# Convolution halves delayed, block sums written earlier, and one block fewer in the second up group of an encoder trunk

## The chip, the cores and the metric

The kernel runs on one core of one Trainium2 chip. The metric is the device time of one execution in microseconds; lower is better. TensorE is called PE here, VectorE DVE, ScalarE ACT, GpSimd POOL and SyncE SP, as in the profile.

## The reference, cut to what matters

Two encoder layers over 256 tokens of 2048 features. Each has an attention mixer and then a gated feed-forward network with a convolution along the tokens; the change touches only the latter.

```python
D_MODEL = 2048; SEQ = 256; DEPTH = 2; D_FF = 5632; CONV_W = 3
...
def conv_ffn(x, w_up, conv_w, conv_b, w_down):
    h = jnp.einsum("bsd,df->bsf", x, w_up)
    g, u = h[..., :D_FF], h[..., D_FF:]
    gp = jnp.pad(g, ((0, 0), (1, 1), (0, 0)))
    g = conv_w[0] * gp[:, :-2] + conv_w[1] * gp[:, 1:-1] + conv_w[2] * gp[:, 2:] + conv_b
    return jnp.einsum("bsf,fd->bsd", jax.nn.gelu(g) * u, w_down)
...
for layer in range(DEPTH):
    ...
    f = conv_ffn(rmsnorm(h, ln_ffn[layer]), ffn_w_up[layer], ffn_conv_w[layer],
                 ffn_conv_b[layer], ffn_w_down[layer])
    h = h + f.astype(h.dtype)
```

## The kernel before, in words

**Products in three matmuls.** Every float32 operand is split into a rounded high part and the rest, the low part. A product is high x high, high x low and low x high: three matmuls (L195 to L197, or `products`, L874 to L877). A weight comes in units of 256 rows by 512 columns: SP loads it into `raw` (a ring of 5 buffers, L124), ACT casts it into `wh`, DVE subtracts and writes `wl` (rings of 4; `split`, L230 to L234). A unit makes 12 matmuls of 512 columns: two row tiles, two token halves, three matmuls each.

**Up groups.** The 5632 gate and 5632 value columns are worked off in 11 groups `j` of 512 and 512 (`up_group`, L922). In a group the first half, `x = 0`, makes the gate columns in two PSUM banks, one for each 128 tokens, and the second half, `x = 1`, the value columns. When a half is done, ACT writes it scaled into `z` (L953), DVE turns `z` in 32 x 32 pieces (L279) and 16 small DMAs, four from SP and twelve from POOL, move the pieces to their places, so that features lie on the partitions (`qk`).

**Blocks.** In groups 1 to 10 the units `u` of `UPK` (1 and 3) don't go as plain units. `up_front` (L844) makes for each of them a block of 2 x 2 tiles with seven products instead of eight: `front_forms` (L887) loads the unit's gate and value weights, DVE makes sums of them (L894 to L901), and four products go into four banks of the next group while the current group still runs (`block`, L850; 12 matmuls). `merged` (L858) then adds these banks up (DVE L862 to L866, ACT L861 and L865) and writes the sums back as the starting values of the next group. That group begins with `up_direct` (L915), which loads the unit's value weight once more and adds the three products left (9 matmuls). The first block is called as `up_front` starts, in the gate half before the third last unit, the second at the same place of the value half.

**The order of the work.** `later(delay, fn)` puts a function off by so many ticks; `tick()` (L98) is called after every second unit and runs what is due. The convolution of a group (`convolved`, L963) is done in two halves of two feature tiles: ACT makes the middle tap and the bias (L971), DVE adds the other two taps (L972, L974), ACT takes the gelu (L977). It needs the gate half's `qk`. `multiplied` (L1001) then multiplies gate and value (L1004) and splits the products for the down projection. The program is written in this order, and a scheduler then places the instructions of each engine; an engine does what it has in its fixed order, so an instruction that waits holds up all behind it.

**Down projection.** Groups 0 to 5 and 6 to 10 make two halves of a layer (`HALVES`), and after each the products are multiplied by the down weights (`pair_head`, L1075), with blocks of their own (`column_forms`, L1012; `seven_products`, L1042). So the last group of a half, 5 or 10, finishes its convolution and `multiplied` during `pair_head`. There are four such ends in the kernel.

Of the kernel before, what the change touches and what calls it, by code (L numbers as in the profile page):

```python
# [48 lines left out]
AHEAD = 4  # L49
LAST = 2  # L50
UPK = (1, 3)
HALVES = ((0, 6, (1, 2, 3)), (6, 11, (1, 2, 3)))


# [17 lines left out]
def trunk_kernel(ctx: ExitStack, tc, a, out):  # L72
# [21 lines left out]
    def later(delay, fn, rank=2):  # L94

        pending.append((now[0] + delay, rank, fn))
# [212 lines left out]
    def turned_rows(c, gain, res):  # L309
# [6 lines left out]
        def tiles():  # L316
            for j in range(4):
                res[c * 4 + j] = y_tile(pf.rearrange("p (t j) q -> p j t q", t=2)[:, j], gain, c * 4 + j)
            for n, u in enumerate(UPK):
                if res is formed.get("of") and c == u // 2:  # L320
# [240 lines left out]
    ps = tps("s", 2)  # L561
# [273 lines left out]
    for pair in range(2):  # L835
        ps, vt = gemm_a(a["evb_v"][pair], yT, KT), []
# [7 lines left out]
    def up_front(layer, j, yT):  # L844

        gm = (j >= HALVES[0][1]) == j % 2
        b1, b7, b6, b5 = (tps(*(("gm", 4) if gm else (tag, 2))) for tag in ("s", "s", "tp", "tp"))
        direct = []

        def block(n):  # L850
            u = UPK[n]
            w11, t1, t2, t3, t4 = front_forms([a["up"][layer, j, x] for x in range(2)], u, j)
            s1, s2, s3, s4 = formed[u]
            for ps, form, w in ((b1, token_block(yT, 2 * u, 0), w11), (b7, s3, t3), (b6, s2, t2), (b5, s1, t1)):
                products(ps, form, w, n == 0, u == UPK[-1])
            direct.append((u, s4, t4))

        def merged():  # L858

            s1, x0, x1 = (tmp.tile([P, 512], F32, name=nm("sum"), tag=tag) for tag in ("rx", "ry", "ry"))  # L860
            S.copy(s1, b1)  # L861
            V.tensor_tensor(x0, s1, b6, op=ALU.add)  # L862
            V.tensor_tensor(x1, x0, b7, op=ALU.add)
            V.tensor_tensor(b6, x0, b5, op=ALU.add)
            S.copy(b7, x1)  # L865
            V.tensor_tensor(b5, x1, b5, op=ALU.add)  # L866

        block(0)
        return [[b1, b7], [b6, b5]], direct, merged, block

    def token_block(act, kt, t):
        return [act[kt][:, x, t * P:(t + 1) * P] for x in range(2)]
# [1 line left out]
    def products(ps, form, w, first=False, last=False, onto=False):  # L874
        (ah, al), (wh, wl) = form, w
        for i, (x, y) in enumerate(((ah, wh), (ah, wl), (al, wh))):
            T.matmul(ps, x, y, start=first and i == 0, stop=last and i == 2, skip_group_check=onto)  # L877
# [44 lines left out]
    def up_group(layer, j, yT, rstd, prod, front, after, *more):  # L922

        sides = {}
        src = [a["up"][layer, j, x] for x in range(2)]
        if front:
            pss, direct = front[:2]
            units = [u for u in range(8) if u not in UPK]
            for u, s4, t4 in direct:
                up_direct(pss, src, yT, u, s4, t4)  # L930
        else:
            pss = [[tps("gm", 4), tps("gm", 4)] for _ in range(2)]
            units = list(range(8))
        nxt = None
        for x in range(2):
            for n, u in enumerate(units):
                if not j and not x and u == 2:
                    rstd.append(row_factor())
                if not x and u == units[-3] and after:
                    nxt = up_front(*after)  # L940
                if x and nxt and u == units[-3]:
                    nxt[3](1)
                if front:
                    own_unit(pss[x], src[x], u, yT, u == units[-1])
                else:
                    a_unit(pss[x], src[x], u, yT, KT)
                if n % 2 == 1 or n == len(units) - 1 and n % 2 == 0:
                    tick()
            if x and nxt:
                nxt[2]()  # L950
            z = new_z("f k")
            for t in range(2):
                S.activation(z.rearrange("p (f t) k -> p t f k", t=2)[:, t],  # L953
                             pss[x][t].rearrange("p (f k) -> p f k", k=P), AF.Copy, scale=rstd[0][:, t:t + 1])
            sides[x] = quad(2 * x)
            turned(z.rearrange("p b k -> p (b k)"), sides[x].rearrange("p f (t k) -> p (f t) k", k=P), (3,))
            if not x:
                later(2, lambda: convolved(layer, j, sides, 0))
                later(4, lambda: convolved(layer, j, sides, 1))
        later(3, lambda: multiplied(j, sides, prod, *more))  # L960
        return nxt

    def convolved(layer, j, sides, part):  # L963

        if not part:
            sides[2] = quad(4)
        g4, c4 = sides[0], sides[2]
        for i in (2 * part, 2 * part + 1):
            f = 4 * j + i
            g, c = g4[:, i, :], c4[:, i, :]  # L970
            S.activation(c, g, AF.Identity, scale=convw[:, layer, 1, f:f + 1], bias=convb[:, layer, f:f + 1])  # L971
            V.scalar_tensor_tensor(c[:, 1:SEQ], g[:, 0:SEQ - 1], convw[:, layer, 0, f:f + 1],  # L972
                                   c[:, 1:SEQ], op0=ALU.mult, op1=ALU.add)
            V.scalar_tensor_tensor(c[:, 0:SEQ - 1], g[:, 1:SEQ], convw[:, layer, 2, f:f + 1],  # L974
                                   c[:, 0:SEQ - 1], op0=ALU.mult, op1=ALU.add)
        half = c4[:, 2 * part:2 * part + 2, :]
        S.activation(half, half, AF.Gelu_apprx_tanh)  # L977
# [115 lines left out]
    def chunk_pair(src, c, act, forms, nk, done, after=None):  # L1093

        nu = nk // 2
        nxt = None
        heads = nu - 3 if nu > 10 else nu - 2
        pss = pair_head(src, c, act, forms, sorted(forms), heads, nk)
        if not c:
            flush()  # L1100
        for x in range(2):
            for u in range(heads, nu):
                if not x and u == nu - 1 and after:
                    nxt = up_front(*after)
                if x and nxt and u == nu - 2:
                    nxt[3](1)
                a_unit(pss[x], src[c + x], u, act, nk)
            if x and nxt:
                nxt[2]()
            if c:  # L1110
                tick()
            done(pss[x], c + x)
        return nxt
# [111 lines left out]
    ps = gemm_a(a["odc"][0], yT, KT, hooks={6: flush})  # L1225
# [10 lines left out]
    for n in range(2):  # L1236
        ps = gemm_a(a["odc"][1 + n], yT, KT)
# [6 lines left out]
    for hh in range(2):  # L1244
        vt = v_tiles(gemm_a(a["od_v"][hh], yT, KT), rstd, ((18, 19, 20, 21), (16, 17, 22, 23))[hh])
        for hd in range(hh * 4, hh * 4 + 4):
            y = att.tile([P, 6, 64], F32, name=nm("nb"), tag="bias", bufs=2)
# [167 lines left out]
def _paired_up(w):  # L1415

    w = w.copy()
    for u in UPK:
        x, y = w[:, 1:, 0, u].copy(), w[:, 1:, 1, u].copy()
        w[:, 1:, 0, u] = np.concatenate([x[..., :512], y[..., :512]], axis=-1)  # L1420
        w[:, 1:, 1, u] = np.concatenate([y[..., 512:], x[..., 512:]], axis=-1)
    return w


# [69 lines left out]
```

## Time and profile before

| | |
|---|---|
| median of 3 runs | 2425.67 us (2424.55 to 2427.95) |
| profiled execution | 2421.42 us |
| its span, first to last instruction | 2419.6 us |
| granted PE clock, mean | 0.997 |
| PE busy | 2386.3 us, 10841 matmuls |
| DVE, ACT, POOL busy | 1874.3, 1409.4, 537.4 us |
| weights and the rest from HBM | 479.46 MB, 199 GB/s over the span |

Rows of a timeline hold the start in us, the duration, the engine, the source line, the operation, what it writes and reads, its shape and count, and in brackets the idle time of the engine before it with what ended that. Rows of one kind that follow each other are merged and counted (x4). SPq is SP's queue, in which DMAs are started. Rows of waits read: who waited, for whom, total us, times, the longest. Rows of windows read: the window, its length, then busy time and count of PE, of its weight loads, of DVE, ACT and POOL, then the granted clock, the share of the DMA engines, and GB/s.

### The profile page before, as it was taken

The page shows a single profiled execution, that of the slowest core. Times are in us where ns is not written, and L with a number is a line of the kernel's source. Part 1 is how long each engine was busy: PE and PEld are TensorE (multiplying, and loading weights), DVE is VectorE, ACT ScalarE, POOL GpSimd, SP SyncE. Part 2 cuts the span into 40 slices and gives each one's busy share as a digit, 9 for nine tenths or more (in the row PEclk, how much of TensorE's full clock was granted, in tenths as well). Part 3 has the DMA queues.
Part 4 walks back from the last instruction along what each step waited for, and adds up shares of the span by engine and source line. Part 5 has one row for each costly group of instructions (what it writes and reads, how often), then busy time and mean ns, then how long its engine had stood idle before and what let it go on. Part 6 is the DMA issues. An engine that isn't in the chain of part 4 may idle for free.

```text
span 2419.6 us, 33368 instructions
## 1 busy us (share of the span) xinstructions
PE 2386.3 (99%) x10841; PEld 1974.4 (82%) x10841; DVE 1874.3 (77%) x2525; ACT 1409.4 (58%) x2078; POOL 537.4 (22%) x940
## 2 busy tenths in 40 slices
PE   9999999999999999999999999999999999999998
PEld 7888888888877887888887888888788878887877
DVE  6576566766778987798978867777788877989787
ACT  7455455566656665456655667555566554566554
POOL 1132032322222332002331200322223320033310
PEclk9999999999999999999999999999999999999999
DMA  8778678766767887678877754667688866788864
GB/s 307 204 194 238 199 193 239 219 195 188 218 203 245 246 248 201 199 231 247 250 227 202 234 183 141 196 192 218 194 254 244 251 192 200 234 236 242 244 202 156
DMA packets 293295, 526.65 MB, mean 218 GB/s; under 512 B 159736, under 2 KB 161144, under 8 KB 293120
## 3 DMA queue, kind: packets, MB, share of 16 engines
q1 hardware_dynamic: 262608, 491.12, 64.7%
q0 software_dynamic: 30080, 32.74, 7.9%
q8 instruction: 85, 1.39, 0.2%
q14 instruction: 90, 0.74, 0.1%
q10 hardware_dynamic: 432, 0.66, 0.1%
HBM read 479.46 MB, written 2.18 MB: 199 GB/s over the span
## 4 chain that ended last, share of the span: by engine, by line
PE 65%; DMA 12%; DVE 11%; issue 4%; POOL 4%; ACT 2%; SPq 2%; DVEq 0%; ACTq 0%; POOLq 0%
PE gm L196 14%; PE gm L195 14%; PE gm L197 14%; DMA qk<-z 9%; PE gm L877 5%; DVE wl L234 5%; PE s L877 4%; POOL qk L273 4%; PE tp L877 3%; PE gm L145 2%; DMA raw<-in_up 2%; SPq L273 2%; DVE z L279 1%; PE gm L150 1%; DVE qk L972 1%
## 5 line engine op out<-in xcount | busy, mean ns | idle before, releaser
L231 ACT CAST wh<-raw 128x1024 fp32r<-128x1024 f32 (+1 forms) x915 | 931.2, 1027 | 680.5 <-PE gm L197 346.4
L234 DVE TENSOR_TENSOR wl<-raw,wh 128x1024 fp32r<-128x1024 f32 (+1 forms) x915 | 1080.2, 1194 | 285.1 <-ACT wh L231 275.3
L273 POOL DMA_DIRECT2D qk<-z x656 | 377.3, 583 | 1129.4 <-DVE z L279 1079.9
L196 PE MATMUL gm<-wl,yT 128*128 128x512 f32 x988 | 385.5, 390 | 1.6 <-DVE wl L234 1.6
L195 PE MATMUL gm<-wh,yT 128*128 128x512 f32 x988 | 386.7, 392 | 0.0
L197 PE MATMUL gm<-wh,yT 128*128 128x512 f32 x988 | 385.3, 390 | 0.0
L877 PE MATMUL gm<-wh,yT 128*128 128x512 f32 x832 | 265.8, 390 | 0.0
L877 PE MATMUL s<-wh,yT 128*128 128x512 f32 x672 | 218.5, 390 | 0.0
L196 PEld LDWEIGHTS gm<-wl,yT 128*128 128x128 f32 x988 | 185.7, 188 | 39.9 <-DVE wl L234 2.7
L197 PEld LDWEIGHTS gm<-wh,yT 128*128 128x128 f32 x988 | 185.5, 188 | 39.0 <-DVE yT L240 0.2
L195 PEld LDWEIGHTS gm<-wh,yT 128*128 128x128 f32 x988 | 185.6, 188 | 37.8 <-issue 0.4
L196 PE MATMUL gm<-wl,prod 128*128 128x512 f32 x518 | 204.3, 394 | 9.3 <-DVE wl L234 9.3
L195 PE MATMUL gm<-wh,prod 128*128 128x512 f32 x518 | 203.6, 393 | 2.8 <-ACT wh L231 2.8
L197 PE MATMUL gm<-wh,prod 128*128 128x512 f32 x518 | 203.4, 393 | 0.0
L877 PEld LDWEIGHTS gm<-wh,yT 128*128 128x128 f32 x832 | 156.2, 188 | 32.9
L877 PE MATMUL tp<-wh,yT 128*128 128x512 f32 x576 | 180.6, 389 | 0.0
L877 PE MATMUL gm<-wl,yT 128*128 128x512 f32 x416 | 162.6, 391 | 0.7 <-DVE wl L234 0.7
L877 PEld LDWEIGHTS s<-wh,yT 128*128 128x128 f32 x672 | 126.2, 188 | 26.7
L877 PE MATMUL s<-wl,yT 128*128 128x512 f32 x336 | 131.4, 391 | 0.0
L877 PEld LDWEIGHTS tp<-wh,yT 128*128 128x128 f32 x576 | 108.1, 188 | 22.4
L196 PEld LDWEIGHTS gm<-wl,prod 128*128 128x128 f32 x518 | 98.3, 190 | 32.4 <-DVE wl L234 12.0
L195 PEld LDWEIGHTS gm<-wh,prod 128*128 128x128 f32 x518 | 98.2, 190 | 24.6 <-ACT wh L231 4.0
(386 smaller groups left out, 3645.9 us busy)
## 6 DMA issues: line engine op xcount, KB each, us to landing
raw<-in_up SPq DMA_DIRECT2D x392, 512.0 KB, 4.9
raw<-in_down SPq DMA_DIRECT2D x176, 512.0 KB, 4.4
raw<-in_eva_qk SPq DMA_DIRECT2D x96, 512.0 KB, 4.4
raw<-in_eva_v SPq DMA_DIRECT2D x46, 512.0 KB, 5.9
qk<-z POOLq DMA_DIRECT2D x656, 32.0 KB, 3.9
raw<-in_evb_qk SPq DMA_DIRECT2D x32, 512.0 KB, 4.7
raw<-in_ev_out SPq DMA_DIRECT2D x32, 512.0 KB, 4.2
raw<-in_od_qk SPq DMA_DIRECT2D x32, 512.0 KB, 4.3
```

The costliest lines, as they stand in the source:

```text
L145: T.matmul(ps.rearrange("p a b -> p (a b)"), wh[:, k * P:(k + 1) * P], act[u * 8 + k].rearrange("p a b -> p (a b)"), start=(u == 0 and k = ...
L150: T.matmul(ps[:, 1, :], wl[:, k * P:(k + 1) * P], act[u * 8 + k][:, 0, :], start=False, stop=(u * 8 + k == KT - 1))
L195: T.matmul(ps[t], ah, wh[:, sl], start=(kt == 0), stop=False)
L196: T.matmul(ps[t], ah, wl[:, sl], start=False, stop=False)
L197: T.matmul(ps[t], al, wh[:, sl], start=False, stop=(kt == nk - 1))
L231: first = S.copy(dst_h, src)
L234: V.tensor_tensor(dst_l, src, dst_h.bitcast(F32), op=ALU.subtract)
L273: (nc.sync if i in on_sync else G).dma_start(dst[j * 32:(j + 1) * 32, :, i * 32:(i + 1) * 32], z[i * 32:(i + 1) * 32].rearrange("p (b j c) ...
L279: V.transpose(p, p)
L877: T.matmul(ps, x, y, start=first and i == 0, stop=last and i == 2, skip_group_check=onto)
L972: V.scalar_tensor_tensor(c[:, 1:SEQ], g[:, 0:SEQ - 1], convw[:, layer, 0, f:f + 1], c[:, 1:SEQ], op0=ALU.mult, op1=ALU.add)
```

## The change

Three edits. First, a function `blocks(j)` takes the place of `UPK`: group 1 has one block, of unit 3, and unit 1 is a plain unit of it; its block is made in the value half of group 0, and nothing in the gate half. Group 1 has seven plain units in each half then, and four ticks instead of three. Second, `merged` is called before the tick behind the last unit of the value half instead of after it, ahead of what that tick has due. Third, the two halves of the convolution are due 3 and 4 ticks after the gate half instead of 2 and 4, and 4 and 5 in the last group of a half.

```diff
+def blocks(j):
+    return () if j == 0 else UPK[1:] if j == 1 else UPK
...
+        us = blocks(j)
+
         def block(n):
-            u = UPK[n]
+            u = us[n]
...
-                products(ps, form, w, n == 0, u == UPK[-1])
+                products(ps, form, w, n == 0, u == us[-1])
...
-        block(0)
-        return [[b1, b7], [b6, b5]], direct, merged, block
+        return [[b1, b7], [b6, b5]], direct, merged, block, len(us)
...
-            units = [u for u in range(8) if u not in UPK]
+            units = [u for u in range(8) if u not in blocks(j)]
...
                     nxt = up_front(*after)
+                    if nxt[4] > 1:
+                        nxt[3](0)
                 if x and nxt and u == units[-3]:
-                    nxt[3](1)
+                    nxt[3](nxt[4] - 1)
...
-                if n % 2 == 1 or n == len(units) - 1 and n % 2 == 0:
+                if x and nxt and u == units[-1]:
+                    nxt[2]()
+                if n % 2 == 1 or u == units[-1]:
                     tick()
-            if x and nxt:
-                nxt[2]()
...
-                later(2, lambda: convolved(layer, j, sides, 0))
-                later(4, lambda: convolved(layer, j, sides, 1))
+                for part in range(2):
+                    later(part + (3 if after else 4), lambda part=part: convolved(layer, j, sides, part))
```

The weights are stored accordingly (`_paired_up`), and `chunk_pair` calls the first block of group 6 itself.

What it does to the order is shown by the rows of the instructions as they are placed. The lines of the change are 4 to 9 higher; L978 to L984 are its convolution, L1011 its product of gate and value, L1034 to L1038 its sums of down weights. Numbers behind a name are buffers.

First place: DVE at the end of the first half of layer 0, where the convolution of group 5 (`qk`) and the turn of its values (`z`) stand beside the first down weights (`raw`, `wl`). Before:

```order
L234 TENSOR_TENSOR wl_8506<-raw_8503,wh_8505 128x1024
L972 SCALAR_TENSOR_TENSOR qk_8416<-qk_8326,convw,qk_8416 128x255
L974 SCALAR_TENSOR_TENSOR qk_8416<-qk_8326,convw,qk_8416 128x255
L972 SCALAR_TENSOR_TENSOR qk_8416<-qk_8326,convw,qk_8416 128x255 x2
L974 SCALAR_TENSOR_TENSOR qk_8416<-qk_8326,convw,qk_8416 128x255 x2
L972 SCALAR_TENSOR_TENSOR qk_8416<-qk_8326,convw,qk_8416 128x255
L1027 TENSOR_TENSOR t_1576_8619<-raw_8615 128x512
L974 SCALAR_TENSOR_TENSOR qk_8416<-qk_8326,convw,qk_8416 128x255
L234 TENSOR_TENSOR wl_8531<-raw_8528,wh_8530 128x1024
L279 STREAM_TRANSPOSE z_8460<-z_8460 128x1024
```

With the change:

```order
L238 TENSOR_TENSOR wl_8485<-raw_8482,wh_8484 128x1024
L979 SCALAR_TENSOR_TENSOR qk_8500<-qk_8313,convw,qk_8500 128x255
L981 SCALAR_TENSOR_TENSOR qk_8500<-qk_8313,convw,qk_8500 128x255
L979 SCALAR_TENSOR_TENSOR qk_8500<-qk_8313,convw,qk_8500 128x255
L981 SCALAR_TENSOR_TENSOR qk_8500<-qk_8313,convw,qk_8500 128x255
L238 TENSOR_TENSOR wl_8511<-raw_8508,wh_8510 128x1024
L1034 TENSOR_TENSOR t_1571_8606<-raw_8602 128x512
L283 STREAM_TRANSPOSE z_8439<-z_8439 128x1024
L238 TENSOR_TENSOR wl_8529<-raw_8526,wh_8528 128x1024
L979 SCALAR_TENSOR_TENSOR qk_8500<-qk_8313,convw,qk_8500 128x255 x2
L981 SCALAR_TENSOR_TENSOR qk_8500<-qk_8313,convw,qk_8500 128x255 x2
```

The second half of the convolution has moved behind one weight, the turn of `z` and another weight. A little further on in the same place, before:

```order
L1031 TENSOR_TENSOR raw_8616<-raw_8616 128x512
L234 TENSOR_TENSOR wl_8629<-raw_8615,wh_8628 128x1024
L1027 TENSOR_TENSOR t_1593_8701<-raw_8697 128x512
L234 TENSOR_TENSOR wl_8637<-raw_8616,wh_8636 128x1024
L1004 TENSOR_TENSOR qk_8416<-qk_8416,qk_8463 128x1024
L1028 TENSOR_TENSOR raw_8697<-raw_8698,raw_8697 128x512
L234 TENSOR_TENSOR wl_8664<-raw_8661,wh_8663 128x1024
```

With the change:

```order
L1038 TENSOR_TENSOR raw_8603<-raw_8603 128x512
L238 TENSOR_TENSOR wl_8616<-raw_8602,wh_8615 128x1024
L1034 TENSOR_TENSOR t_1588_8688<-raw_8684 128x512
L1011 TENSOR_TENSOR qk_8500<-qk_8500,qk_8442 128x1024
L238 TENSOR_TENSOR wl_8624<-raw_8603,wh_8623 128x1024
L238 TENSOR_TENSOR prod_8588<-qk_8500,prod_8588 128x256 x2
L238 TENSOR_TENSOR prod_8593<-qk_8500,prod_8593 128x256 x2
L238 TENSOR_TENSOR wl_8651<-raw_8648,wh_8650 128x1024
```

The product of gate and value now comes before the weight that follows the subtraction, and the four splits of the products before the next weight. The other three ends have the same order.

Second place: DVE from group 1 to group 2 of layer 0; `sum` and `gm` are the sums of group 2's blocks, `wl_6946` before and `wl_6940` now are its first direct weight. Before:

```order
L862 TENSOR_TENSOR sum_6914<-sum_6913,gm_6638 128x512
L234 TENSOR_TENSOR wl_6898<-raw_6895,wh_6897 128x1024
L863 TENSOR_TENSOR sum_6915<-sum_6914,gm_6637 128x512
L864 TENSOR_TENSOR gm_6638<-sum_6914,gm_6639 128x512
L866 TENSOR_TENSOR gm_6639<-sum_6915,gm_6639 128x512
L234 TENSOR_TENSOR wl_6946<-raw_6943,wh_6945 128x1024
L972 SCALAR_TENSOR_TENSOR qk_6869<-qk_6744,convw,qk_6869 128x255 x2
L974 SCALAR_TENSOR_TENSOR qk_6869<-qk_6744,convw,qk_6869 128x255 x2
```

With the change:

```order
L868 TENSOR_TENSOR sum_6901<-sum_6900,gm_6607 128x512
L238 TENSOR_TENSOR wl_6885<-raw_6882,wh_6884 128x1024
L979 SCALAR_TENSOR_TENSOR qk_6874<-qk_6713,convw,qk_6874 128x255 x2
L981 SCALAR_TENSOR_TENSOR qk_6874<-qk_6713,convw,qk_6874 128x255 x2
L869 TENSOR_TENSOR sum_6902<-sum_6901,gm_6606 128x512
L870 TENSOR_TENSOR gm_6607<-sum_6901,gm_6608 128x512
L872 TENSOR_TENSOR gm_6608<-sum_6902,gm_6608 128x512
L979 SCALAR_TENSOR_TENSOR qk_6874<-qk_6713,convw,qk_6874 128x255 x2
L981 SCALAR_TENSOR_TENSOR qk_6874<-qk_6713,convw,qk_6874 128x255 x2
L238 TENSOR_TENSOR wl_6940<-raw_6937,wh_6939 128x1024
```

Both halves of group 1's convolution now stand before the direct weight, and the first of them before three of the sums.

Third place: DVE from group 0 to group 1 of layer 0. Before:

```order
L972 SCALAR_TENSOR_TENSOR qk_6400<-qk_6310,convw,qk_6400 128x255
L974 SCALAR_TENSOR_TENSOR qk_6400<-qk_6310,convw,qk_6400 128x255
L972 SCALAR_TENSOR_TENSOR qk_6400<-qk_6310,convw,qk_6400 128x255
L862 TENSOR_TENSOR sum_6523<-sum_6522,tp_6217 128x512
L974 SCALAR_TENSOR_TENSOR qk_6400<-qk_6310,convw,qk_6400 128x255
L863 TENSOR_TENSOR sum_6524<-sum_6523,s_6216 128x512
L864 TENSOR_TENSOR tp_6217<-sum_6523,tp_6218 128x512
L866 TENSOR_TENSOR tp_6218<-sum_6524,tp_6218 128x512
L234 TENSOR_TENSOR wl_6555<-raw_6552,wh_6554 128x1024
```

With the change:

```order
L868 TENSOR_TENSOR sum_6482<-sum_6481,tp_6217 128x512
L979 SCALAR_TENSOR_TENSOR qk_6437<-qk_6276,convw,qk_6437 128x255
L869 TENSOR_TENSOR sum_6483<-sum_6482,s_6216 128x512
L870 TENSOR_TENSOR tp_6217<-sum_6482,tp_6218 128x512
L872 TENSOR_TENSOR tp_6218<-sum_6483,tp_6218 128x512
L981 SCALAR_TENSOR_TENSOR qk_6437<-qk_6276,convw,qk_6437 128x255
L979 SCALAR_TENSOR_TENSOR qk_6437<-qk_6276,convw,qk_6437 128x255
L238 TENSOR_TENSOR wl_6521<-raw_6518,wh_6520 128x1024
```

The sums begin before the second half of the convolution instead of within it; one step of it stands behind the direct weight.

More of the change, by code (lines that the diff above doesn't have):

```diff
@@ L1104, in chunk_pair @@
                     nxt = up_front(*after)
+                    nxt[3](0)
                 if x and nxt and u == nu - 2:
@@ L1417, in _paired_up @@
     w = w.copy()
[L1418 to L1421, printed above, removed]
+    for j in range(w.shape[1]):
+        for u in blocks(j):
+            x, y = w[:, j, 0, u].copy(), w[:, j, 1, u].copy()
+            w[:, j, 0, u] = np.concatenate([x[..., :512], y[..., :512]], axis=-1)
+            w[:, j, 1, u] = np.concatenate([y[..., 512:], x[..., 512:]], axis=-1)
     return w
```

## The prediction

> **What bounds the kernel now.** I read the page first, then PE's waits, then the stretches by window, and last the timelines of PE, ACT, DVE and SP where PE waits.
>
> ```profile
> span 2419.6 us, 33368 instructions
> PE 2386.3 (99%) x10841; PEld 1974.4 (82%) x10841; DVE 1874.3 (77%) x2525; ACT 1409.4 (58%) x2078; POOL 537.4 (22%) x940
> PE gm L196 <- DVE wl L234: 11.6, 10, 1.8
> 1956.00:1966.00 10.00, 7.39 (x25) 5.40 (x24) 10.00 (x15) 7.74 (x11) 4.79 (x9) 0.83 0.49 95
> 2306.00:2317.00 11.00, 8.13 (x22) 6.24 (x23) 10.47 (x15) 7.29 (x10) 6.23 (x11) 0.69 0.50 112
> ```
>
> PE is busy 99% of the span, so time is lost only in single waits. The third line (source, what it waited for, us, times, longest) says what for: the low part of a weight that DVE subtracts. The last two lines (PE, PEld, DVE and ACT busy, then the granted clock) are stretches with such waits in which the clock fell as well. The profiled execution took 2421.42 us, 1.8 us more than its span and 4.25 us less than the median of the runs, 2425.67.
>
> The same thing happens at the end of every half of a layer, at four places. Here is the first, on PE, then ACT, DVE and SP:
>
> ```profile
> 921.32 0.39 PE L195 MATMUL gm<-wh,prod 128*128 128x512 f32 x1
> ...
> 926.76 0.39 PE L195 MATMUL gm<-wh,prod 128*128 128x512 f32 x1
> 927.74 0.50 PE L196 MATMUL gm<-wl,prod 128*128 128x512 f32 x1 [0.59 <-DVE wl L234]
> ...
> 943.09 0.50 PE L1054 MATMUL tp<-wl,form 128*128 128x512 f32 x1 [0.73 <-DVE wl L234]
> ...
> 946.49 0.51 PE L196 MATMUL gm<-wl,prod 128*128 128x512 f32 x1 [1.75 <-DVE wl L234]
> ...
> 955.92 0.50 PE L1054 MATMUL tp<-qk,form 128*128 128x512 f32 x1 [0.25 <-DVE qk L234]
> ```
>
> ```profile
> 921.94 2.08 ACT L971 ACTIVATE qk<-qk,convb,convw 128x256 f32<-128x256 f32 x4 [4.81 <-DMA qk<-z]
> 924.50 1.04 ACT L231 CAST wh<-raw 128x1024 fp32r<-128x1024 f32 x1
> ```
>
> ```profile
> 922.57 0.48 DVE L972 SCALAR_TENSOR_TENSOR qk<-qk,convw,qk 128x255 f32<-128x255 f32 x1 [4.18 <-ACT qk L971]
> ...
> 926.46 1.22 DVE L234 TENSOR_TENSOR wl<-raw,wh 128x1024 fp32r<-128x1024 f32 x1
> 927.59 1.24 DVE L279 STREAM_TRANSPOSE z<-z 128x1024 f32<-128x1024 f32 x1
> ...
> 941.20 0.69 DVE L1027 TENSOR_TENSOR t<-raw 128x512 f32<-128x512 f32 x1 [4.06 <-DMA raw<-in_down]
> 941.81 1.22 DVE L234 TENSOR_TENSOR wl<-raw,wh 128x1024 fp32r<-128x1024 f32 x1
> 943.47 1.22 DVE L1004 TENSOR_TENSOR qk<-qk,qk 128x1024 f32<-128x1024 f32 x1 [0.44 <-issue]
> ...
> 945.22 1.22 DVE L234 TENSOR_TENSOR wl<-raw,wh 128x1024 fp32r<-128x1024 f32 x1
> ```
>
> ```profile
> 928.86 2.55 SPq L273 DMA_DIRECT2D qk<-z  x4
> 931.52 1.27 SPq L128 DMA_DIRECT2D raw<-in_down  x2
> 932.91 0.39 SPq L1015 DMA_DIRECT2D raw<-in_down  x1
> ```
>
> 24 matmuls of 512 columns start in 926.76 - 921.32 us, so one costs 0.227 us, not its 0.39 of duration. ACT stands 4.81 us before the convolution's first step, whose gates, transposed and moved by DMA, have not landed, and every cast of a weight stands behind it. DVE then runs all eight steps of the convolution (922.57 to 926.46 with one subtraction of a weight between) before the weight that PE wants at 926.99. That is the first wait. DVE's backlog delays z, SP's four moves of z stand ahead of the next weights, and 13 us later DVE waits 4.06 us for a weight; PE waits twice more, until 946.49, and shortly at 955.92.
>
> **The change part by part.**
>
> *One block instead of two in group 1.* Per layer PE loses 12 matmuls of the block and 9 of its direct products, and gains 24 of two plain units: 3 more, 6 in all, 6 x 0.227 = **+1.4 us**. PE is the bound, so nothing hides them. In return DVE does 7 steps fewer a layer and SP starts one load fewer, and the block's two loads no longer stand in group 0's queue. PE has no wait there in this trace, so that saving is hidden behind PE and I take it at nothing; what it could do for the stream of loads is a rival.
>
> *Sums ahead of due work, group 0 to group 1.*
>
> ```profile
> 707.56 1.08 ACT L971 ACTIVATE qk<-qk,convb,convw 128x256 f32<-128x256 f32 x2
> 708.55 0.56 ACT L861 COPY sum<-s 128x512 f32<-128x512 f32 x1
> 709.50 0.68 DVE L862 TENSOR_TENSOR sum<-sum,tp 128x512 f32<-128x512 f32 x1
> 712.28 2.35 DVE L234 TENSOR_TENSOR wl<-raw,wh 128x1024 fp32r<-128x1024 f32 x2
> 713.56 0.50 PE L877 MATMUL tp<-wl,form 128*128 128x512 f32 x1 [1.16 <-DVE wl L234]
> ```
>
> In the new order ACT copies the sum before the second pair of convolution steps, so at 707.56, done at 708.1. Four sums at 0.6 apart and the three steps left at 0.4 then bring DVE to the weight, done at 708.1 + 2.4 + 1.2 + 1.2 = 712.9 instead of 713.45: 0.55 us of PE's wait goes, in both layers **-1.1 us** (0 if the sums come no earlier).
>
> *The same edit and the later halves, group 1 to group 2.* With a second plain unit, group 1's second half is longer, and the new order has the convolution ahead of the direct block's weight, where it stood behind it.
>
> ```profile
> 736.90 0.69 ACT L953 ACTIVATE z<-s,rstd 128x512 f32<-128x512 f32 x1 [0.67 <-PE s L877]
> 750.86 1.22 DVE L234 TENSOR_TENSOR wl<-raw,wh 128x1024 fp32r<-128x1024 f32 x1
> 755.04 0.98 DVE L972 SCALAR_TENSOR_TENSOR qk<-qk,convw,qk 128x255 f32<-128x255 f32 x2 [2.96 <-DMA raw<-in_up]
> 755.74 0.39 PE L877 MATMUL gm<-wh,form 128*128 128x512 f32 x1
> PE gm L877 <- DVE wl L234: 0.7, 1, 0.7
> ```
>
> The gate half ends on PE at about 736.75, where z could start. Six units of 12 matmuls and a block of 12 later, 84 x 0.227 = 19.1 us, PE begins the direct products (755.74); the weight was made at 750.86. Now PE comes there 7 units and a block, 96 x 0.227 = 21.8 us after the gate half, and needs the weight's low part at 22.0. DVE starts the convolution, if its gates land as before, at 755.04, 18.3 us after the gate half, and puts four steps (1.7), three sums (1.8), four steps (1.6) and the weight (1.2) in a row: 24.5 us. ACT's cast of the same weight stands behind its own four steps too, but ends before the sums do. PE, with the direct products of two blocks queued behind the one that waits, stands 2.4 us, in two layers **+4.8 us**. Ends: 0, if the gates land 2.5 us sooner, to +3 a layer. In the first layer a later wait of 0.7 (last line, between 755 and 800 us) has that slack, **-0.7 us**.
>
> *The halves one tick later, at the four ends.* Now four steps stand before the weight and four behind z. DVE gets to the weight after 1.7 us instead of 3.9, so 2.2 us sooner, at 925.5 done: the wait at 926.76 goes. ACT's pair, cast and z let DVE turn z at 926.0 instead of 927.59, so SP's moves and the weights behind them start 1.6 us sooner, and the weight at 941.20, which lands behind those in one stream, at 939.6. POOL's twelve moves of the same z keep their order and start 1.6 us sooner as well. But there the new order is worse: behind that subtraction now stand L1004, the weight, the four products and the next weight (0.6 + 1.1 + 1.1 + 1.4 + 1.2 = 5.4 us), where the last low part was done 946.44 - 941.20 = 5.2 us behind it. At the first place L1004 waits for its own z besides: it started at 943.47, so now at 941.9, and what stands from there to the second weight takes 4.8 us, to 946.7 and not 946.44. PE's first wait is given back to the later ones (2.7 and 1.1 us, 1.4 apart, in place of 0.9 and 1.9): 0.25 us lost, 0.4 gained at 955.92, for which the weights now stand earlier, 0.2 us gained in all. The other places:
>
> ```profile
> 1285.16 0.69 DVE L1027 TENSOR_TENSOR t<-raw 128x512 f32<-128x512 f32 x1 [4.05 <-DMA raw<-in_down]
> 1288.64 1.22 DVE L234 TENSOR_TENSOR wl<-raw,wh 128x1024 fp32r<-128x1024 f32 x1
> 1973.43 0.69 DVE L1027 TENSOR_TENSOR t<-raw 128x512 f32<-128x512 f32 x1 [4.13 <-DMA raw<-in_down]
> 1976.92 1.22 DVE L234 TENSOR_TENSOR wl<-raw,wh 128x1024 fp32r<-128x1024 f32 x1
> 2309.38 0.80 PE L196 MATMUL gm<-wl,prod 128*128 128x512 f32 x1 [1.66 <-DVE wl L234]
> 2322.25 0.69 DVE L1027 TENSOR_TENSOR t<-raw 128x512 f32<-128x512 f32 x1 [2.21 <-DMA raw<-in_down]
> 2327.95 0.39 PE L196 MATMUL gm<-wl,prod 128*128 128x512 f32 x1
> ```
>
> At the second and third the weight was done 4.7 us behind the subtraction; 5.4 us behind one that is 1.6 us sooner gains 0.9 each, and 0.4 for the short wait behind. At the fourth the first wait, ended at 2309.38, ends 1.9 us sooner, and the second barely takes from it (2322.25 - 1.6 + 5.4 = 2326.05, against PE's 2327.95, the row that wanted that weight). Sum 0.2 + 1.3 + 1.3 + 1.9 = **-4.7 us**. Ends: 0, if the weight lands no sooner, to -8, if the second waits shrank like the first. Between, from group 2's value half to group 4 and in groups 6 to 9, the order does not move, so the edits cost and gain nothing there.
>
> Sum: 1.4 - 1.1 + 4.8 - 0.7 - 4.7 = -0.3 us, 2421.1 against 2421.42 of the profiled execution, and with the same difference against the median **2425.4 us**: no change.
>
> **A rule weighed.** The clock fell to 0.69 around 2306 to 2317, though no wait of L196 in PE's list passed 1.8 us: the one of 1.66 us at 2309.38 stood close behind another. The new order makes the second waits longer (2.7 and 1.1 us at the first end). The Trainium skill, TensorE: Matmul & The Clock Gate, Part 1, lets the clock fall only after an idle window of about 3.4 us; no wait that I expect is as long, so by the page it never falls at the ends and the sum stays. The trace disagrees with its number and decides: a fall is a rival.
>
> **The rivals.** *Slower, A: the weights land no sooner.* The load that DVE waits for at 941.20 reuses a buffer that the moved order frees no earlier than before. If it is its own issue that counts and not the stream ahead of it, the ends give 0: 1.4 - 1.1 + 4.8 - 0.7 = +4.4, with 3 instead of 2.4 us at group 2 +5.6: 2431.3 us. It decides from under 0.5 us of shift. For it: SP starts that load at 932.91 now, and in the new order I get 932.8. Against: two loads were started within 1.27 us ahead of it, and DVE had it only 8.3 us after its start, so they come one behind the other. Chance 0.18. *Slower, B: the clock falls* at three of four ends, 2 us each (0.31 of the clock over the 11 us of the window above would be 3.4, half of it behind waits): -0.3 + 6 = +5.7, 2431.4 us. Chance 0.08. *Faster: no wait at group 2*, because the gates land sooner with a weight less in the stream, -4.8: -5.1, 2420.6 us. Chance 0.22. *The change does nothing* is inside the forecast, 0.52.
>
> **How the numbers follow.** Two measurements tell about 0.2% apart, 4.9 us. The rivals' ends give the chances: faster 0.22, same 0.52, slower 0.26. The range reaches from 2418 (the faster rival with 2 us more at the ends) to 2432 (A with a fall of the clock).
>
> **What would show it.** PE's list: the wait at the first low part of each end gone, the one at L1054 about 2 us, and a new wait of about 2.4 us on `gm<-wl,form` at group 2. ACT's 4.8 us before the convolution stays. Wrong would be: group 2 without a wait, the subtraction at the ends as late as now, or a clock under 0.9 at three ends.

## The result, and the profile after

The changed kernel takes 2435.72 us (median of 5 runs, 2432.66 to 2440.45) against 2425.67 us before. The ratio of the runs is 1.0053, 95% interval 1.0037 to 1.0069. A second set of runs (e9 below) gave 2435.03 against 2422.60 us, ratio 1.0050 (1.0033 to 1.0066). So the change costs 10 to 12 us where the prediction had 0 and reached up to 2432. Single runs of one kernel lie up to 15 us apart (before, in the 30 runs beside e1 to e4: 2415.95 to 2431.40), so medians of many runs and ratios decide, and a single profile is good for the place of a loss, not for its last microsecond.

The head of the page after, and its list of PE's waits (source, what it waited for, total us, times, longest):

```profile
span 2433.7 us, 33342 instructions
PE 2392.7 (98%) x10847; PEld 1978.6 (81%) x10847; DVE 1867.5 (77%) x2511; ACT 1406.4 (58%) x2072; POOL 538.7 (22%) x940
```

```profile
PE tp L1061 <- DVE wl L238: 6.4, 4, 2.9
PE gm L200 <- DVE wl L238: 6.4, 8, 1.2
PE gm L882 <- DVE wl L238: 5.9, 3, 2.7
PE tp L882 <- DVE wl L238: 5.3, 5, 1.8
PE gm L882 <- DVE gm L870: 3.4, 2, 2.4
```

PE has the six matmuls more. L200 (the L196 of before) waits half as long, L1061 (L1054) four times as long (6.4 us in four waits, where about 2 us each were forecast); new are 5.9 + 3.4 us on `gm` at L882, the direct products of group 2.

To see where the time went I take, for every matmul of a trace, the distance to the next one's start less the median distance for its width (0.227 us at 512 columns), and add this up over stretches between the same points of the program. The same points are the same matmuls in the order of the program, which hardly differs between the kernels. What PE loses so contains its waits and the slower pace behind them, in us:

| | group 0 to 1, both layers | group 1 to 2, both layers | four half-ends | the rest | all |
|---|---|---|---|---|---|
| before | 5.5 | 2.1 | 23.1 | 23.0 | 53.7 |
| after | 5.8 | 13.9 | 20.9 | 25.7 | 66.3 |
| after, again (e9) | 7.1 | 14.0 | 20.2 | 24.3 | 65.6 |

12.6 us of loss and 6 x 0.227 = 1.4 us of matmuls make 14.0 of the 14.1 us between the two spans. 11.8 of them lie at one place: the end of group 1. There, in the first layer, on PE, DVE and ACT of the changed kernel:

```profile
755.13 0.39 PE L882 MATMUL tp<-wh,yT 128*128 128x512 f32 x1
757.91 0.47 PE L882 MATMUL gm<-wh,form 128*128 128x512 f32 x1 [2.40 <-DVE gm L870]
761.13 0.80 PE L882 MATMUL gm<-wl,form 128*128 128x512 f32 x1 [2.74 <-DVE wl L238]
```

```profile
737.19 0.69 DVE L900 TENSOR_TENSOR raw<-raw,raw 128x512 f32<-128x512 f32 x1 [0.92 <-DMA raw<-in_up]
...
738.53 1.24 DVE L283 STREAM_TRANSPOSE z<-z 128x1024 f32<-128x1024 f32 x1
...
748.66 1.23 DVE L238 TENSOR_TENSOR wl<-raw,wh 128x1024 fp32r<-128x1024 f32 x1 [1.03 <-ACT wh L235]
754.80 0.98 DVE L979 SCALAR_TENSOR_TENSOR qk<-qk,convw,qk 128x255 f32<-128x255 f32 x2 [4.91 <-DMA raw<-in_up]
755.69 0.87 DVE L981 SCALAR_TENSOR_TENSOR qk<-qk,convw,qk 128x255 f32<-128x255 f32 x2
756.49 0.68 DVE L869 TENSOR_TENSOR sum<-sum,gm 128x512 f32<-128x512 f32 x1
757.08 0.69 DVE L870 TENSOR_TENSOR gm<-sum,gm 128x512 f32<-128x512 f32 x1
757.68 0.69 DVE L872 TENSOR_TENSOR gm<-sum,gm 128x512 f32<-128x512 f32 x1
758.28 0.87 DVE L979 SCALAR_TENSOR_TENSOR qk<-qk,convw,qk 128x255 f32<-128x255 f32 x2
759.07 0.87 DVE L981 SCALAR_TENSOR_TENSOR qk<-qk,convw,qk 128x255 f32<-128x255 f32 x2
759.86 3.49 DVE L238 TENSOR_TENSOR wl<-raw,wh 128x1024 fp32r<-128x1024 f32 x3
```

```profile
733.80 0.69 ACT L960 ACTIVATE z<-s,rstd 128x512 f32<-128x512 f32 x1 [0.17 <-PE s L882]
...
754.16 2.08 ACT L978 ACTIVATE qk<-qk,convb,convw 128x256 f32<-128x256 f32 x4 [5.53 <-DMA qk<-z]
```

DVE stands idle 4.91 us and ACT 5.53 us for the gates of group 1. (The bracket of DVE's row names a load of `raw`; but the step reads what ACT's first tap writes, and that starts at 754.16.) Behind DVE's first step stand the sums that PE needs at 755.36 (PE waits 2.40 us) and, further back, the low part of the direct weight (2.74 us more). The windows behind it (length; busy time and count of PE, PEld, DVE, ACT, POOL; granted clock; DMA share; GB/s), at the place in the first layer and in the second:

```profile
755.00:765.00 10.00, 4.86 (x13) 3.38 (x12) 9.99 (x16) 8.80 (x13) 0.21 (x1) 0.74 0.31 99
1795.00:1805.00 10.00, 6.26 (x21) 4.58 (x20) 9.99 (x16) 9.01 (x13) 0.00 (x1) 0.83 0.32 105
```

PE is busy 4.9 and 6.3 of 10 us, and its clock falls to 0.74 and 0.83, where before it had 10.00 of 10.00 and 1.00 in both.

### The profile page after: what moved, and what is told of

It is laid out like the page before. It is cut to its first block, busy times and chain, and to the rows that moved or that the text cites. A ratio compares the mean times of both kernels' runs of the same rounds, so it can differ in the third digit from the quotient of the medians.

```text
span 2433.7 us, 33342 instructions
## 1 busy us (share of the span) xinstructions
PE 2392.7 (98%) x10847; PEld 1978.6 (81%) x10847; DVE 1867.5 (77%) x2511; ACT 1406.4 (58%) x2072; POOL 538.7 (22%) x940
## 5 line engine op out<-in xcount | busy, mean ns | idle before, releaser
L200 PE MATMUL gm<-wl,yT 128*128 128x512 f32 x988 | 385.1, 390 | 1.7 <-DVE wl L238 1.7
L882 PE MATMUL gm<-wh,yT 128*128 128x512 f32 x832 | 266.8, 391 | 0.0
L882 PE MATMUL s<-wh,yT 128*128 128x512 f32 x680 | 221.0, 391 | 0.0
L200 PEld LDWEIGHTS gm<-wl,yT 128*128 128x128 f32 x988 | 185.6, 188 | 39.5 <-DVE wl L238 2.4
L200 PE MATMUL gm<-wl,prod 128*128 128x512 f32 x518 | 203.3, 393 | 4.7 <-DVE wl L238 4.7
L882 PE MATMUL tp<-wh,yT 128*128 128x512 f32 x592 | 185.5, 389 | 0.0
L882 PEld LDWEIGHTS gm<-wh,yT 128*128 128x128 f32 x832 | 157.0, 189 | 33.2
L882 PE MATMUL gm<-wl,yT 128*128 128x512 f32 x416 | 162.7, 391 | 0.0
L882 PEld LDWEIGHTS s<-wh,yT 128*128 128x128 f32 x680 | 128.3, 189 | 27.4
L882 PE MATMUL s<-wl,yT 128*128 128x512 f32 x340 | 133.4, 392 | 0.3 <-DVE wl L238 0.2
L882 PEld LDWEIGHTS tp<-wh,yT 128*128 128x128 f32 x592 | 111.1, 188 | 23.0
L200 PEld LDWEIGHTS gm<-wl,prod 128*128 128x128 f32 x518 | 97.7, 189 | 28.1 <-DVE wl L238 7.6
L882 PE MATMUL tp<-wl,yT 128*128 128x512 f32 x296 | 115.3, 389 | 0.9 <-DVE wl L238 0.9
```

What stands on the lines that cost most here:

```text
L200: T.matmul(ps[t], ah, wl[:, sl], start=False, stop=False)
```

## The experiments

All times are medians in us; beside each stands before from the same call, then the ratio with its interval. "Edits" are numbered as in the section on the change: 1 one block, 2 early sums, 3 late halves.

| run | what it has | time | before | ratio | lost from group 1 to 2 | at the ends |
|---|---|---|---|---|---|---|
| e1 | edit 1 | 2432.39 | 2424.78 | 1.0029 (1.0019 to 1.0040) | 10.4 | 20.8 |
| e2 | edit 3 | 2418.89 | 2424.78 | 0.9978 (0.9966 to 0.9989) | 1.0 | 21.1 |
| e3 | edits 2, 3 | 2420.27 | 2424.78 | 0.9988 (0.9975 to 1.0000) | 3.5 | 22.6 |
| e4 | change, group 1's halves at 5 and 6 | 2433.96 | 2424.78 | 1.0036 (1.0022 to 1.0050) | 9.9 | 25.7 |
| e5 | e4 with the taps pinned | 2422.03 | 2425.26 | 0.9993 (0.9982 to 1.0004) | 0.6 | 25.7 |
| e6 | edits 1, 3 | 2432.83 | 2425.26 | 1.0040 (1.0023 to 1.0056) | 11.5 | 17.8 |
| e7 | edits 1, 2 | 2434.36 | 2425.26 | 1.0039 (1.0024 to 1.0055) | 13.9 | 21.3 |
| e8 | edit 2 | 2424.15 | 2425.26 | 0.9996 (0.9986 to 1.0005) | 2.8 | 24.7 |
| e9 | the change again | 2435.03 | 2422.60 | 1.0050 (1.0033 to 1.0066) | 14.0 | 20.2 |
| e10 | e5 without edit 3 | 2423.29 | 2422.60 | 1.0000 (0.9990 to 1.0011) | 0.2 | 23.7 |
| e11 | e2, group 0's halves at 5 and 6, pinned | 2412.85 | 2422.60 | 0.9956 (0.9940 to 0.9972) | 1.1 | 14.9 |
| e12 | e2, halves at 5 and 6 at the ends | 2423.02 | 2422.60 | 1.0000 (0.9989 to 1.0012) | 0.8 | 23.6 |
| e13 | e11 without edit 3 | 2413.57 | 2423.08 | 0.9952 (0.9935 to 0.9969) | 0.1 | 19.6 |
| e14 | e11 again | 2411.15 | 2423.08 | 0.9953 (0.9940 to 0.9966) | 0.1 | 18.0 |

**e1, edit 1 alone.** `merged` behind the tick, `later(2, ...)` and `later(4, ...)` as before.

> Only the first edit: one block in group 1; the sums behind the tick and the halves of the convolution at 2 and 4 ticks, as before. Theory P (the place): the loss of the change lies at the end of group 1, where the convolution now stands ahead of the block's sums and of the direct block's weight on DVE, and it is this edit that puts it there; in the trace of the change PE loses 6.6 us more there than before in each layer (waits of 2.6 and 3.0 in the first, 1.2 and 3.0 in the second, and a lower clock behind them). It expects 1.4 + 2 x 6.6 = 14.6 us above before in the profile, 10 to 15 in the median, 2436 to 2441, and two long waits at that place in each layer. Rival E (the ends): the later halves of the convolution make the new waits of 3.1 us and less behind the half-ends; then this kernel costs its 6 matmuls, 2427. Rival S (the stream of loads): one block less shifts all loads that follow, and the loss is spread over many small waits; then 2431 to 2436 without long waits at the end of group 1.

7.6 us slower, with two waits at the place in each layer (2.44 and 0.90 us, 0.43 and 1.16 us); PE loses 10.4 us there, 8.3 more than before. Edit 1 makes the loss. The total came out under the bracket of theory P and in that of rival S, but the loss lies at one place and not spread over many waits.

**e2, edit 3 alone.**

```diff
-    return () if j == 0 else UPK[1:] if j == 1 else UPK
+    return () if j == 0 else UPK
...
-                if x and nxt and u == units[-1]:
-                    nxt[2]()
                 if n % 2 == 1 or u == units[-1]:
                     tick()
+            if x and nxt:
+                nxt[2]()
```

> Only the third edit: the halves of the convolution one tick later or more; two blocks in group 1, sums behind the tick. The order of the instructions differs from before at the four half-ends alone. Theory P: in the traces the change loses 1.0 and 1.0 us more at the first two ends and 0.9 and 3.6 less at the last two, 2.5 us less in all: 2421 to 2425.5, and no long wait at the end of group 1. Rival E: 8 to 10 us above before, 2434. The prediction's own term was 4.7 us less, 2421.

5.9 us faster, close to the term of 4.7; rival E is out. But its trace loses 21.1 us at the ends against 23.1, so the gain isn't seen where it was forecast; e13 comes back to this.

**e3, two blocks.** The first two lines of e2's diff alone.

> The changed kernel with two blocks in group 1 again: the second and third edits. Theory P: the end of group 1 has the old order, its two long waits are gone and the clock stays, and the 6 matmuls go: 14.6 us less than the change in the profile, 2421 to 2425 in the median. Rival E: the ends are as in the change, 2434. Rival S: 2425 to 2428, what the ends bring being noise.

4.5 us faster than before, 15 less than the change: with the second block back the loss at the place is gone but for 1.4 us.

**e4, the halves of group 1 two ticks later.**

```diff
-                    later(part + (3 if after else 4), lambda part=part: convolved(layer, j, sides, part))
+                    later(part + (5 if j == 1 else 3 if after else 4), lambda part=part: convolved(layer, j, sides, part))
```

> The changed kernel with one block in group 1, but that group's two halves of the convolution due 5 and 6 ticks after the gate half instead of 3 and 4: on DVE and ACT the block's sums and the direct block's weight stand ahead of the convolution again. PE's and SP's order is that of the change, word for word. Theory P: no wait of over 1 us at the end of group 1, no fall of the clock there, 13 us less than the change: 2423 to 2426. Rival E: as the change, 2435. Rival S: as the change or up to 3 us less, 2432 to 2435, since the loads and their order are the same.

2433.96, the number of rival S. The trace says why. ACT of e4, then its PE:

```profile
754.38 0.60 ACT L978 ACTIVATE qk<-qk,convb,convw 128x256 f32<-128x256 f32 x1 [5.76 <-DMA qk<-z]
754.88 1.03 ACT L235 CAST wh<-raw 128x1024 fp32r<-128x1024 f32 x1
```

```profile
755.97 0.50 PE L882 MATMUL gm<-wh,form 128*128 128x512 f32 x1 [0.74 <-ACT wh L235]
```

The scheduler had put ACT's first tap ahead of the cast of the direct weight all the same, where it waits 5.76 us for the gates. The wait had only moved from DVE to ACT, and PE's losses were spread over several weights (0.9, 1.0, 0.8, 0.6 and 0.9 us from 754 to 783 are the five largest). So e4 does not separate theory P from rival S; e5 does.

**e5, pinned on ACT as well.** Added to e4:

```diff
-            S.activation(c, g, AF.Identity, scale=convw[:, layer, 1, f:f + 1], bias=convb[:, layer, f:f + 1])
+            tap = S.activation(c, g, AF.Identity, scale=convw[:, layer, 1, f:f + 1], bias=convb[:, layer, f:f + 1])
+            if j == 1:
+                tc.keep_in_program_order(tap)
```

> As e4, but the taps of group 1's convolution are pinned on ACT behind the casts that the program writes before them. In e4 the sums and the weight stood ahead of the convolution on DVE alone: on ACT the first tap, waiting for its gates until 754.38, still stood ahead of the cast of the direct block's weight (754.88), so e4 moved the wait and didn't take it away; its text was wrong in that. Here the convolution stands behind the direct weight and the weights of two units on both engines. Theory P (the place: DVE's and ACT's wait for the gates at the end of group 1 is what the change loses): no wait of over 1 us at the direct products of group 2, clock 1.00 from 745 to 765, 2423 to 2428. Rival S (with one block less the stream of weights runs late from group 1 on, wherever the convolution stands): waits of 0.5 to 1 us in a row from 755 to 785 stay, as in e4, and 2432 to 2435.

2422.03 us: with PE's and SP's order of the change, 13.0 us less than e9 (2435.03), and 0.6 instead of 14.0 us lost at the place. Theory P is shown, and rival S is out. DVE and ACT of e5, and its two windows:

```profile
751.29 0.68 DVE L869 TENSOR_TENSOR sum<-sum,gm 128x512 f32<-128x512 f32 x1
751.89 0.69 DVE L870 TENSOR_TENSOR gm<-sum,gm 128x512 f32<-128x512 f32 x1
752.49 0.69 DVE L872 TENSOR_TENSOR gm<-sum,gm 128x512 f32<-128x512 f32 x1
753.09 1.22 DVE L238 TENSOR_TENSOR wl<-raw,wh 128x1024 fp32r<-128x1024 f32 x1
```

```profile
751.85 1.05 ACT L235 CAST wh<-raw 128x1024 fp32r<-128x1024 f32 x1 [1.73 <-DMA raw<-in_up]
...
758.91 1.10 ACT L978 ACTIVATE qk<-qk,convb,convw 128x256 f32<-128x256 f32 x2
```

```profile
755.00:765.00 10.00, 10.00 (x45) 8.25 (x44) 7.88 (x10) 5.79 (x9) 3.29 (x6) 1.00 0.80 245
1795.00:1805.00 10.00, 10.00 (x45) 8.26 (x44) 9.93 (x15) 6.17 (x11) 6.89 (x12) 1.00 0.85 217
```

The sums and the weight are done at 754.3, the tap starts at 758.91 without a wait, PE has no gap, and the clock stays at 1.00.

**e6, edits 1 and 3**, and **e7, edits 1 and 2.**

> The first and third edits, the sums behind the tick as before. The first edit alone cost 7 us, the third alone brought 6, the second and third together brought 4. Theory I (the early sums and the one block work against each other: with both, the second half of the sums and the direct weight stand behind the first half of the convolution): without the early sums the parts add, 2424.8 + 7 - 6 = 2426. Rival H (the later halves and the one block work against each other, since the later halves are written behind a group that has a tick more): 2432 to 2436. Rival A (all parts add and the change's own measurement is high): 2426 here, and 2434 in e7.

> The first and second edits, the halves of the convolution at 2 and 4 ticks. The order at the end of group 1 is that of the change. Theory I: 1.5 and 2.5 us more of waits there than with the block alone, by the traces, and the clock: 2437 to 2441. Rival H: 2432. Rival A: 2424.8 + 7 + 2 = 2434.

2432.83 and 2434.36: e6 lies in the bracket of rival H, e7 at the number of rival A, and neither in that of theory I. Beside edit 1 the late halves bring nothing (e6 against e1). The early sums add 1.5 us to e1; the traces show 13.9 us at the place in e7 and in the change against 10.4 and 11.5 in e1 and e6. That is in the direction of theory I, but smaller than its bracket, and in time not beyond the intervals. The three edits don't add: 7.6 - 5.9 - 1.1 = +0.6 against +10 to +12 for the change.

**e8, edit 2 alone.**

> The second edit alone. The prediction expected 1.1 us less, from group 0 to group 1. Theory I: within 2 us of before, since with two blocks the order at the end of group 1 doesn't move: 2423 to 2427. Rival A: e3 less e2, 2 us above before, 2427.

1.1 us less, the term of the prediction to the digit, which is luck: its interval holds no change at all, and from group 0 to 1 its trace loses 6.8 us against 5.5 before. The one wait that was priced did shrink: PE's 1.16 us before the low part of the direct weight is 0.80 here, 0.77 and 0.80 in the change, 0.4 less a layer where 0.55 were forecast. But the waits just ahead of it differ by more from trace to trace.

**e9, the change again**, and **e10, e5 with the old halves elsewhere.**

> The changed kernel as it is, beside the same runs of before as e10 to e12. Theory P, by the traces of the change and of e5: PE loses 8.3 and 5.7 us around the end of group 1 against 0.5 and 0.1, so 13 us above e5: 2434 to 2437. Rival A (the parts add, and its first five runs were high): 7 - 6 - 1 us against before, 2425 to 2428.

> e5 with the halves of the convolution at 2 and 4 ticks again in all other groups, so that the four half-ends have the order of before. The prediction's term for the ends, 4.7 us, and e2, 6 us less than before: 4 to 6 us above e5, 2426 to 2428. Rival N (the ends gain nothing: in the traces PE loses 21 to 23 us over the four ends with the halves early, 18 to 23 with the halves late, 26 in e5): as e5, 2421 to 2424.

e9 confirms the result. e10 is 0.7 us above before where e5 is 3.2 below, by the ratios 1.7 us apart; the late halves are worth that or less here, and rival N's bracket holds.

**e11, the same cure between groups 0 and 1.** e2 with

```diff
-                    later(part + (3 if after else 4), lambda part=part: convolved(layer, j, sides, part))
+                    later(part + (5 if j == 0 else 3 if after else 4), lambda part=part: convolved(layer, j, sides, part))
...
+            if j == 0:
+                tc.keep_in_program_order(tap)
```

> e2 with the convolution of group 0 due 5 and 6 ticks after the gate half and its taps pinned on ACT: at the end of group 0 too the sums and the direct weights stand ahead of it on both engines. Theory P, taken to another place: PE loses 2.9 and 4.1 us there in the trace of e2; about 1 stays in each layer, so 4 to 5 us less than e2: 2413 to 2416. Rival S (the weights come as they come): as e2, 2418 to 2420.

2412.85 us, 9.8 less than before and faster than both kernels. Before, ACT's first tap waited ahead of the casts at the end of group 0 too; in e11 nothing waits there. ACT of before, ACT of e11, and the window in both, before first:

```profile
702.73 1.10 ACT L971 ACTIVATE qk<-qk,convb,convw 128x256 f32<-128x256 f32 x2 [3.93 <-DMA qk<-z]
```

```profile
711.52 1.10 ACT L978 ACTIVATE qk<-qk,convb,convw 128x256 f32<-128x256 f32 x2
```

```profile
695.00:715.00 20.00, 18.41 (x79) 14.48 (x78) 13.63 (x21) 14.44 (x20) 2.08 (x4) 1.00 0.63 191
```

```profile
695.00:715.00 20.00, 20.00 (x90) 16.52 (x89) 14.69 (x20) 11.54 (x14) 3.52 (x7) 1.00 0.87 259
```

PE's 7.0 us of loss there in e2 become 0.1. The time came out just under theory P's bracket. In the traces of e11, e13 and e14 the four ends lose 15 to 20 us instead of 21 to 23 as well; why they do wasn't tried.

**e12, two ticks later at the ends.** In e2 `4` becomes `5` for the last group of a half.

> e2 with the halves 5 and 6 ticks after the gate half in the last group of a half instead of 4 and 5. If DVE's steps ahead of the first down weight are what the first wait of an end is for, the waits of 0.9 and 1.4 us that e2 still has there go, 2 to 4 us less than e2: 2415 to 2417. Rival: the second wait at L1061 (2.0 to 2.7 us in e2) takes it over, or the products come late for the down projection: 2419 to 2425.

2423.02, no better than before, 4.1 above e2 though in another call. Its rival held: PE's waits at L1061 are 3.52, 2.98, 0.63 and 2.81 us at the four ends, where e2 has 2.40, 1.83, 2.48 and 2.52.

**e13 and e14, the late halves once more.** e13 is e11 with `part + 5 if j == 0 else 2 * part + 2`.

> e11 with the halves of the convolution at 2 and 4 ticks in the groups behind group 0, so that the four half-ends have the order of before. If the later halves bring what the prediction gave the ends, 4 to 6 us above e14. If the waits at the ends only move from the first low part to the next ones, within 2 us of e14.

> The kernel of e11 again, beside e13: 2411 to 2415, 9 to 11 us less than before.

0.9952 and 0.9953, in medians 2413.57 and 2411.15. Where nothing else differs, the late halves bring 0 to 2.4 us. At the ends e13 loses 19.6 us in its trace, e14 18.0 and e11, the same kernel as e14, 14.9. With e6 and e10 that makes three comparisons near nothing against one (e2) of 5.9. Two more are on record: beside edit 2 the late halves bring 1.9 us by the ratios (e3 against e8), beside edits 1 and 2 they cost 2.7 to 3.4 (the change and e9 against e7). What e2 shows beyond this stays unexplained; its interval reaches down to 2.7 us.

## Why the prediction was wrong

**The step that failed** is the one of group 1 to group 2: "DVE starts the convolution, if its gates land as before, at 755.04, 18.3 us after the gate half". The place, the order and the steps ahead of the weight were right, and the price was not: +4.8 - 0.7 = +4.1 us forecast, +11.8 in the trace against before, 13.0 between e9 and e5.

The size goes wrong in two pieces. First, the gates land later. Before, the last row of `z` of the gate half starts at 736.90, its turn and the tap are

```profile
739.46 1.24 DVE L279 STREAM_TRANSPOSE z<-z 128x1024 f32<-128x1024 f32 x1
```

```profile
754.40 1.09 ACT L971 ACTIVATE qk<-qk,convb,convw 128x256 f32<-128x256 f32 x2 [4.03 <-DMA qk<-z]
```

so 2.6 and 14.9 us. After, they are 738.53 - 733.80 = 4.7 and 754.16 - 738.53 = 15.6. DVE turns `z` 2.2 us later because its turn stands behind other work: L900 among it, which waits 0.92 us for the second load of the next block. The transfer takes 0.7 us more. So the convolution starts 754.80 - 733.80 = 21.0 us behind `z` and not 18.1. From there to the weight it takes 759.86 + 1.16 - 754.80 = 6.2 us, as forecast (6.3). PE comes to the direct products when it was said to, 21.6 us behind `z`. A wait of 2.4 grows by the 2.9 us to 5.3; measured are 2.40 + 2.74 = 5.1 in the first layer and 1.0 + 2.7 in the second. Why the load comes later in the program, with one direct unit less ahead of it, wasn't tried.

Second, the clock. The prediction had its fall as a rival at the ends and put nothing for it at group 2; it fell here, behind the two waits (0.74 and 0.83 in the windows above). Of the 8.3 us lost in the first layer 5.9 are at the waits and 2.4 behind them, of the 5.7 in the second 4.5 and 1.2.

**Six matmuls, +1.4.** Right: 10847 instead of 10841.

**Sums ahead, -1.1.** The wait that it priced shrank by 0.4 us a layer and not 0.55; in time it is not told from nothing, and where the one block is, the early sums make the place worse (13.9 against 10.4 and 11.5 us).

**The ends, -4.7.** The mechanism shows, the gain mostly doesn't. The first waits shrink but are not all gone: at the four ends PE waits 0.33, 1.76, 0.83 and 0 us there in the change, against 0.59, 1.65, 2.61 and 3.53 before. PE and DVE of e2 at the first end:

```profile
940.43 0.40 PE L1060 MATMUL tp<-wh,form 128*128 128x512 f32 x1
943.22 0.50 PE L1061 MATMUL tp<-wl,form 128*128 128x512 f32 x1 [2.40 <-DVE wl L238]
```

```profile
939.23 0.69 DVE L1034 TENSOR_TENSOR t<-raw 128x512 f32<-128x512 f32 x1 [2.72 <-DMA raw<-in_down]
940.80 1.23 DVE L1011 TENSOR_TENSOR qk<-qk,qk 128x1024 f32<-128x1024 f32 x1 [0.88 <-DMA qk<-z]
941.95 1.22 DVE L238 TENSOR_TENSOR wl<-raw,wh 128x1024 fp32r<-128x1024 f32 x1
943.08 1.42 DVE L238 TENSOR_TENSOR prod<-qk,prod 128x256 fp32r<-128x256 f32 x4
944.42 1.22 DVE L238 TENSOR_TENSOR wl<-raw,wh 128x1024 fp32r<-128x1024 f32 x1
```

The first wait is gone in e2, and the subtraction L1034 starts at 939.23 instead of 941.20, 2.0 us sooner; PE was 0.6 us ahead when the end began, so the edit's part is 1.4 (1.6 forecast). But L1011, now ahead of the weight, waits 0.88 us for its own `z`, and the two low parts are done at 943.2 and 945.6: one wait of 2.4 us at L1061, and 0.13 behind it, in place of three. Behind that wait the clock is at 0.50 for 3.41 us, which it is not at this end before:

```profile
943.92:947.33 3.41, 3.28 (x9) 2.08 (x8) 3.41 (x6) 3.20 (x5) 0.00 (x0) 0.50 0.75 175
```

At half the clock matmuls start 0.427 us apart instead of 0.227, so such a stretch costs up to 1.6 us, about what the shorter waits gained. At this end 4.5 us are lost in both kernels. The prediction saw that here (-0.2 us), but expected 1.3, 1.3 and 1.9 us at the other three, where the traces of before and e2 differ by +0.1, -1.9 and -0.2: at the second end e2 has a fall of the clock that before has not, at the third it is the other way round. The term is 0 to 2.4 us by e13 and e14.

**Of the rivals**, *Faster* (no wait at group 2) was wrong, *A* had the sign, the new wait and ends that bring nothing, and was 4 us too low; *B* had a fall of the clock, but not at group 2. At the ends the change's trace has two (950.91, 1282.00) and before has two as well (1960.29, 2308.45), so there they cost the change nothing more; in e2 they are at three of the four. The sum as the traces of before and after have it is 1.4 + 11.8 + 0.3 (group 0 to 1) - 2.2 (ends) + 2.7 (the rest) = +14.0 us for one profile of each, and 10 to 12 by the medians.

## What to carry to other kernels

Before an instruction that waits for a DMA is moved by a delay or a cut in the work, list on every engine it touches what stands behind it in the queue and when PE wants that; the price is the whole of that lateness and what the clock then costs, and it has to be counted from the turn of the data on its engine, not from when its input is ready. Writing an instruction later in the program need not place it later: the scheduler put a tap that waits 5.76 us for a transfer ahead of a cast that PE was about to need (e4; why it does so is not shown). So look at the order on both engines (e4 fixed one and gained nothing), and pin it behind the work that is due (e5, e11). What a kernel loses elsewhere for the same reason can be worth more than the edit: one pin and a delay of three and two ticks at the end of group 0 brought 9.5 us (e13). Of these 5.4 are lost at that place in the trace of before and not in e13's; where the rest comes from is not shown.

## What the runs showed of the hardware

The clock falls behind short waits, and where they lie counts. In e1 the second layer's place has one matmul between two waits. Below are PE and the windows up to the fall and behind it; then, for comparison, a place in e5 with two waits as close, of 0.97 us (until 1738.43) and 1.16 us (until 1740.10):

```profile
1793.36 0.39 PE L882 MATMUL tp<-wh,yT 128*128 128x512 f32 x1
1794.18 0.47 PE L882 MATMUL gm<-wh,form 128*128 128x512 f32 x1 [0.43 <-ACT qk L984]
1795.81 0.50 PE L882 MATMUL gm<-wl,form 128*128 128x512 f32 x1 [1.16 <-DVE wl L238]
```

```profile
1793.34:1796.76 3.42, 1.83 (x7) 1.02 (x6) 3.42 (x5) 3.42 (x6) 0.00 (x0) 1.00 0.00 0
1796.76:1800.17 3.41, 3.41 (x10) 2.63 (x9) 3.41 (x4) 1.47 (x2) 0.70 (x2) 0.50 0.89 286
```

```profile
1735.63:1739.05 3.42, 2.33 (x10) 1.36 (x8) 1.99 (x5) 2.70 (x4) 0.00 (x0) 1.00 0.06 23
1739.05:1742.46 3.41, 2.36 (x10) 1.99 (x11) 2.81 (x4) 3.38 (x6) 0.00 (x0) 1.00 0.37 102
1742.46:1745.87 3.41, 3.36 (x15) 2.44 (x13) 3.41 (x8) 3.41 (x5) 0.00 (x0) 1.00 0.59 205
```

In e1 the two waits, 1.59 us together, lie in one stretch of 3.41 us, in which PE loses 2.1 us, and the clock is at 0.50 over the next. In e5 the longer waits, 2.13 us together, fall on both sides of 1739.05, 1.5 and 1.2 us are lost, and it stays at 1.00.

The 16 traces agree with this. From 20 to 2400 us they show 52 falls, all to 0.50, each for 3.41 or 6.83 us, and within a trace all begin whole multiples of 3.413 us from one another. I cut each trace into stretches of that length from its falls and counted what PE lost in each: 2.12 us or more was followed by a fall all 46 times, less than 1.95 us never, and what lies between in 6 of 22 cases. This was counted afterwards; no run was made to test it. By it two waits are cheap or dear by where they fall in that grid, and the grid lies differently in two traces of one kernel: the falls at the first end start at 942.09 us in e11 and at 941.29 in e14.

The Trainium skill, TensorE: Matmul & The Clock Gate, Part 1, lets the clock fall after an idle window of about 3.4 us. The length is that of the stretches here, but PE was not idle through the one ahead of the fall in e1 (1.83 us busy), nor is any wait that long there or at the change's place (2.40 and 2.74 us): by the rule as it stands the clock would have stayed at 1.00, and the measurement decides against it.

The spread between runs of one kernel is large beside the effects: up to 15 us, so that e2's 5.9 and e13's 0 to 2.4 for the same edit can both stand.
